# Forgetting scores in pairs of neighbouring PSUM banks: one maximum, one exponential and one sum for a query tile

## The chip, the cores and the metric

The kernel runs on one core of a Trainium2 chip. The time is device microseconds (us) of one execution, and the kernel before takes 1519.09 us, the median of three runs (1518.0 to 1522.42). TensorE (PE) multiplies matrices and writes its products to PSUM, which has eight banks of 128 partitions by 512 float32 numbers. VectorE (DVE) and ScalarE (ACT) read PSUM, GpSimd (POOL) works on SBUF alone, and SyncE (SP) issues the DMAs, in the order of one queue. Each of these engines works through its own instructions in order and waits for others through semaphores.

## The reference

One decoder layer for 1024 tokens of width 1024, all in float32: an mLSTM with 4 heads and forgetting attention with 8 heads of width 64 run side by side on the same normalised input; their outputs are projected, then come cross-attention into 256 memory tokens, a squared-ReLU MLP of width 4096, and a final norm. What the change touches is this:

```python
def forgetting_attention(q, k, v, lf):
    cT = jnp.cumsum(lf, axis=1).transpose(0, 2, 1)
    ...
        s = jnp.einsum('bqhd,bkhd->bhqk', qi, k, preferred_element_type=jnp.float32) * scale
        s = s + (ci[..., :, None] - cT[..., None, :])
        s = jnp.where(qpos[:, None] >= kpos[None, :], s, -jnp.inf)
        p = jax.nn.softmax(s, axis=-1)
        return jnp.einsum('bhqk,bkhd->bqhd', p.astype(v.dtype), v)
```

Queries are taken in tiles of 128. Tile i of a head sees (i + 1) * 128 keys, so the eight tiles of a head are 128, 256, ... 1024 wide.

## The kernel before

A float32 product is made of up to three products of rounded parts: `split` (L135) makes a high part on ACT (L138) and the rest on DVE (L139), and `mm3` (L190) issues the three matmuls (L192, L193, L194). Most of TensorE's time goes to these.

The stages in order: norm and projections; mLSTM heads 0 to 3 (`ml_project`, `ml_head`); the value projection of the forgetting heads (`token_major` with `fv_sink`, L1062); the forgetting heads; the rest of the output projection (`out_rest`); cross-attention; the MLP.

The forgetting heads are written out slot by slot. `slot` (L993) holds, in this order, the work of one step of several pipelines, and `in_order` (L148) ties each compute engine to that order. DMAs and everything outside the slots are placed by the scheduler that builds the program, by its own estimates. A slot has:

- on PE the transposes (`Values.turn`, L793) of up to four 128x128 blocks of probabilities into a `tp` bank (two such banks), with the causal mask (`mask`, L734) added to a score that is waiting for it; then the value products of the step two slots earlier (`Values.add`, L813) into the bank `ov`; then the scores of one part of one query tile (`Tile.score`, L754 and L755) into a bank `sc`; then filling products, below.
- on DVE the negated row maximum (`Tile.top`, L761) of the part scored one slot earlier; the rest of the cut of the transposed block (`Values.cut`, L139); reciprocals of the sums (L775); the sinks of filling products; half of the cuts of weights for these (`cut_half`, L967).
- on ACT the high part of `Values.cut` (L138), then the exponential of the part scored two slots earlier (`Tile.exp`, L767, which also sums), then the high part of a weight cut (L966).
- on POOL the division by the sum (`Tile.scale`, L778) and the other half of the weight cuts (L967).

A tile of up to 512 keys is one part and one `sc` bank; a wider one is two parts (640 keys: 384 and 256; otherwise 512 and the rest), scored in two slots. Each part has its exponential under a maximum of its own: L764 takes the smaller of the two negated maxima for the second part, L769 the factor between the two, L774 joins the sums, and L778 scales both parts. A head has 12 parts, so 12 slots; it has 12 steps of values, too. 13 slots with scores alone go ahead (`LEAD_`), and the values follow from then on, one step a slot.

The filling products (`filler`, L980) are 8 key units, 4 value units (two results each) and 16 units of the output projection, with the cost of a step written as 1.5 or 3.0 (12, 24 and 15 a unit). From the fourth slot with values on, a slot may take steps until the sum of costs reaches 3.6 a slot (L1041), and it stops where a result is complete (L1046 to L1048); the sink of that result runs in the next slot, behind the scores (L1036). Results go in turn to the banks `mm` and `m2`. What is left after the slots runs on its own (L1077).

The eight banks are `sc` x3, `mm`, `m2`, `tp` x2 and `ov`, from the start of the program to its end. The last mLSTM head takes `sc` for its column sums (L615) and for turning its factors into a row (`to_row`, L635); that row goes to DRAM and is read back by L261 and L637. Maxima and sums of a query tile lie in columns with three buffers (`col`, L82).

Of the kernel before, what the change touches and what calls it, by code (L numbers as in the profile page):

```python
# [44 lines left out]
def hybrid_layer(ctx: ExitStack, tc: tile.TileContext, a: dict, out: bass.AP):  # L45
    nc = tc.nc
    v, s, g = nc.vector, nc.scalar, nc.gpsimd

    pool = ctx.enter_context(tc.tile_pool(name="sb", bufs=1))
    psum = ctx.enter_context(tc.tile_pool(name="ps", bufs=1, space=PSUM))  # L50
    dram = ctx.enter_context(tc.tile_pool(name="dr", bufs=1, space=DRAM))

    count = [0]

    def name(tag):
        count[0] += 1
        return f"{tag}_{count[0]}"

    def sb(tag, shape, bufs, dt=F32):
# [25 lines left out]
    PBUFS = dict(sc=3, mm=1, m2=1, tp=2, ov=1)  # L85

    def ps_tile(tag):
        return psum.tile([P, 512], F32, tag=tag, name=name(tag), bufs=PBUFS[tag])

# [485 lines left out]
    mix = dram.tile([2, 2, P, KT, TH], F32, name="mix")  # L575
    facd = dram.tile([MLH, T], F32, name="facd")

    def ml_head(hd, q, k, og, num1, den1):
        fac = col("fac", 8)
        nums = []  # L580
        dens = col("dens", 8)
        sqs = col("sqs", 8)
        for hf in range(2):
# [44 lines left out]
        yield  # L628
        end = hd == MLH - 1
        fbs = [w2("a"), w2("d")] if end else [None, None]  # L630
        at = facd[hd : hd + 1]
        for hf in range(2):
            fb = fbs[hf] or w2("a")
            if hf == 0:
                to_row(fb, fac, 8, at, sc)  # L635
            if hf != end:
                load(fbs[1] or fb, at[:, TH:].broadcast_to([P, TH]))  # L637
# [73 lines left out]

    coming = []

    def fx_load(hd):
# [10 lines left out]
    def fx_step():  # L725
        if coming:
            dst, src = coming.pop(0)
            load(dst.bitcast(F32), src)

    masks = []  # L730

    def mask():
        while masks:
            nc.tensor.matmul(masks.pop(0), identb, causal, start=False, stop=True)  # L734

    class Tile:


        def __init__(self, hd, i, pt):
            self.hd, self.i, self.pt = hd, i, pt  # L740
            self.wid = (i + 1) * P

            step = 384 if self.wid == 640 else TH
            self.parts = [(c0, min(c0 + step, self.wid)) for c0 in range(0, self.wid, step)]
            self.mxs, self.dens = col("mx", 2), col("den", 2)
            self.ps = []

        def score(self, e):
# [3 lines left out]
            c2 = max(c1, c0 + 256)  # L752
            sp = sc()
            nc.tensor.matmul(sp[:, : c2 - c0], qs2[:, it], kl[:, c0:c2], start=True, stop=False)  # L754
            nc.tensor.matmul(sp[:, : c2 - c0], qs[:, it], kh[:, c0:c2], start=False, stop=c1 < self.wid)  # L755
            if c1 == self.wid:
                masks.append(sp[:, c1 - c0 - P : c1 - c0])
            self.ps.append(sp[:, : c1 - c0])

        def top(self, e):  # L760
            v.tensor_reduce(out=self.mxs[:, e : e + 1], in_=self.ps[e], axis=mybir.AxisListType.X, op=ALU.max, negate=True)  # L761
            if e:

                v.tensor_scalar(out=self.mxs[:, 1:2], in0=self.mxs[:, 1:2], scalar1=self.mxs[:, 0:1], scalar2=None, op0=ALU.min)  # L764

        def exp(self, e):
            s.activation(self.pt[:, slice(*self.parts[e])], self.ps[e], AF.Exp, bias=self.mxs[:, e : e + 1], accum_out=self.dens[:, e : e + 1])  # L767
            if e:
                s.activation(self.mxs[:, 0:1], self.mxs[:, 0:1], AF.Exp, bias=self.mxs[:, 1:2], scale=-1.0)  # L769

        def scale(self):
            den = self.dens[:, 0:1]
            if len(self.parts) > 1:
                v.scalar_tensor_tensor(out=den, in0=den, scalar=self.mxs[:, 0:1], in1=self.dens[:, 1:2], op0=ALU.mult, op1=ALU.add)  # L774
            v.reciprocal(den, den)  # L775
            for e, c in enumerate(self.parts):
                x = self.pt[:, slice(*c)]
                g.tensor_scalar(out=x, in0=x, scalar1=den, scalar2=self.mxs[:, 0:1] if e + 1 < len(self.parts) else 1.0, op0=ALU.mult, op1=ALU.mult)  # L778

# [75 lines left out]
    def value_steps():  # L855
        fvs = {0: fv_load(0)}
        for hd in range(FXH):
# [23 lines left out]

    late = []

# [106 lines left out]

    stores, topped = [], []

    def slot(values, until):  # L993
        with in_order():
            todo_ = late[:]
            late.clear()
            closing = bool(ended)
            sums = []
# [10 lines left out]
            while adds and not closing and len(adds) >= (LAG if x else 1):  # L1009
                y = adds.pop(0)  # L1010
                y.add()
                if y.last:
                    ended.append((y.hd, y.hf, y.ov))
                    break
            tops = scored[:]
            scored.clear()
            for t, e in tops:
                t.top(e)
            if x:
                x.cut()  # L1020
                adds.append(x)
            for f in sums:
                f()
            exps = topped[:]
            topped[:] = tops
            for t, e in exps:
                t.exp(e)
            while exped:
                exped.pop(0).scale()
            exped.extend(t for t, e in exps if e == len(t.parts) - 1)  # L1030
# [52 lines left out]
    banks[:] = ["mm", "tp", "m2", "tp"]  # L1083
    mix_fx = [mix_load(MLH + KX, KT, hf) for hf in range(2)]
# [635 lines left out]
```

## Time and profile before

| | |
|---|---|
| median of the runs | 1519.09 us (1518.0 to 1522.42) |
| the profiled execution | 1522.48 us; its span from the first to the last instruction 1520.3 us |
| granted TensorE clock | 0.997 |
| busy, share of the span | PE 99%, its weight loads 83%, DVE 72%, ACT 47%, POOL 29% |
| forgetting heads with values | from 392.3 us to about 579 us of the span |

PE's row counts the matmuls, whose ends are modelled and overlap; a matmul of 512 columns is shown with 0.39 us though the next starts 0.23 us later. So a wait shows as idle time only by what exceeds the matmul's modelled end. A number in square brackets in the list of instructions in order of time is the idle time of that engine before the instruction, with what ended it.

### The profile page before, as it was taken

The numbers are of one execution on the slowest core, as the hardware profiler recorded it, in microseconds if no ns is written. First come the engines' busy times: TensorE is split into PE (matmuls) and PEld (weight loads), VectorE is DVE, ScalarE is ACT, GpSimd is POOL, SyncE is SP. The second block draws the span as 40 slices with busy tenths as digits, with TensorE's granted clock in tenths as the row PEclk, the third lists the DMA queues.
The fourth block names the chain that finished last, engine by engine and source line by source line (L and its number), as shares of the span: only waits on it lengthen the run. The fifth ranks groups of instructions, "written<-read, shape, count | busy, mean of one in ns | idle before, by whom it ended". The sixth has DMA issues, their size and how long they took to land.

```text
span 1520.3 us, 21907 instructions
## 1 busy us (share of the span) xinstructions
PE 1501.2 (99%) x7708; PEld 1259.3 (83%) x7708; DVE 1097.8 (72%) x1741; ACT 717.2 (47%) x1345; POOL 438.5 (29%) x497
## 2 busy tenths in 40 slices
PE   9999999999999999999999999999999999999997
PEld 8888888889898888788888888888888888888887
DVE  7676676665798875844457888788887788777765
ACT  7343343334678763644344456565566432222124
POOL 0003030413455441011110033343344544333312
PEclk9999999999999999999999999999999999999998
DMA  6332333436887968833444436876775975555623
GB/s 206 117 113 91 114 102 124 132 126 172 260 246 222 285 205 313 300 123 122 134 137 157 165 118 237 278 274 243 261 265 214 361 262 222 222 222 215 254 84 111
DMA packets 118097, 296.71 MB, mean 195 GB/s; under 512 B 13138, under 2 KB 27788, under 8 KB 111844
## 3 DMA queue, kind: packets, MB, share of 16 engines
q1 hardware_dynamic: 117700, 295.21, 57.1%
q8 instruction: 60, 0.98, 0.3%
q14 instruction: 49, 0.40, 0.1%
q10 hardware_dynamic: 288, 0.11, 0.0%
HBM read 198.55 MB, written 96.72 MB: 194 GB/s over the span
## 4 chain that ended last, share of the span: by engine, by line
PE 61%; DMA 3%; DVE 2%; issue 1%; ACT 1%; SPq 0%; POOL 0%; POOLq 0%; DVEq 0%; ACTq 0%
PE sc L193 6%; PE sc L192 6%; PE sc L194 6%; PE tp L194 5%; PE tp L192 5%; PE tp L193 5%; PE m L193 4%; PE m L192 4%; PE m L194 4%; PE mm L194 3%; PE mm L193 3%; PE mm L192 3%; PE ov L192 2%; PE ov L194 2%; PE ov L193 2%; PE ov L813 1%
## 5 line engine op out<-in xcount | busy, mean ns | idle before, releaser
L193 PE MATMUL tp<-act,wh 128*128 128x512 f32 (+1 forms) x456 | 178.7, 392 | 0.0
L192 PE MATMUL tp<-act,wl 128*128 128x512 f32 (+1 forms) x456 | 178.5, 392 | 0.0
L194 PE MATMUL tp<-act,wh 128*128 128x512 f32 (+1 forms) x456 | 178.4, 392 | 0.0
L138 ACT ACTIVATE wh<-wr 128x1024 fp32r<-128x1024 f32 (+3 forms) x96 | 92.7, 967 | 99.5 <-PE tp L194 34.1
L139 DVE TENSOR_TENSOR wl<-wr,wh 128x1024 fp32r<-128x1024 f32 (+3 forms) x96 | 112.4, 1172 | 18.7 <-ACT wh L138 18.5
L192 PE MATMUL mm<-act,wl 128*128 128x512 f32 (+1 forms) x320 | 122.8, 384 | 0.0
L193 PE MATMUL mm<-act,wh 128*128 128x512 f32 (+1 forms) x320 | 122.5, 383 | 0.0
L194 PE MATMUL mm<-act,wh 128*128 128x512 f32 (+1 forms) x320 | 122.3, 382 | 0.0
L192 PE MATMUL m<-act,wl 128*128 128x512 f32 (+1 forms) x312 | 119.5, 383 | 2.2 <-DVE r_p L1094 2.2
L193 PE MATMUL m<-act,wh 128*128 128x512 f32 (+1 forms) x312 | 119.0, 382 | 1.0 <-DMA act<-mix 1.0
L194 PE MATMUL m<-act,wh 128*128 128x512 f32 (+1 forms) x312 | 119.0, 381 | 0.0
L192 PE MATMUL sc<-act,wl 128*128 128x512 f32 (+1 forms) x268 | 103.8, 387 | 0.0
L193 PE MATMUL sc<-act,wh 128*128 128x512 f32 (+1 forms) x268 | 103.6, 387 | 0.0
L194 PE MATMUL sc<-act,wh 128*128 128x512 f32 (+1 forms) x268 | 103.6, 387 | 0.0
L194 PEld LDWEIGHTS tp<-act,wh 128*128 128x128 f32 x456 | 85.7, 188 | 19.5
L192 PEld LDWEIGHTS tp<-act,wl 128*128 128x128 f32 x456 | 85.7, 188 | 18.9
L193 PEld LDWEIGHTS tp<-act,wh 128*128 128x128 f32 x456 | 85.8, 188 | 18.8
L1454 POOL TENSOR_TENSOR z<-wr 128x256 f32<-128x256 f32 x56 | 51.7, 944 | 149.3 <-DMA wr<-w_ff2q 107.6
L138 ACT ACTIVATE w<-wr 128x768 fp32r<-128x768 f32 (+2 forms) x31 | 25.5, 825 | 132.1 <-PE tp L194 68.1
L138 ACT ACTIVATE wh<-z 128x1024 fp32r<-128x1024 f32 (+2 forms) x55 | 52.5, 956 | 64.8 <-POOL z L1454 29.3
L139 DVE TENSOR_TENSOR wl<-z,wh 128x1024 fp32r<-128x1024 f32 (+2 forms) x55 | 64.6, 1174 | 11.7 <-ACT wh L138 11.5
L194 PEld LDWEIGHTS mm<-act,wh 128*128 128x128 f32 x320 | 60.1, 188 | 12.5
(679 smaller groups left out, 4199.4 us busy)
## 6 DMA issues: line engine op xcount, KB each, us to landing
act<-right SPq DMA_DIRECT2D x35, 1024.0 KB
right<-r_d SPq DMA_DIRECT2D x70, 256.0 KB
right<-w SPq DMA_DIRECT2D x56, 256.0 KB
wr<-w_ff2q SPq DMA_DIRECT2D x28, 512.0 KB
act<-fqk SPq DMA_DIRECT2D x48, 256.0 KB
wr<-w_in SPq DMA_DIRECT2D x20, 512.0 KB
wr<-w_ff SPq DMA_DIRECT2D x20, 512.0 KB
fqk<-r_p SPq DMA_DIRECT2D x32, 256.0 KB
```

Of the source, the lines that this page charges most:

```text
L138: s.activation(hi, src, AF.Copy)
L139: return v.tensor_tensor(out=lo, in0=src, in1=hi.bitcast(F32), op=ALU.subtract)
L192: nc.tensor.matmul(ps, w[1], x[0], start=first, stop=False, skip_group_check=more)
L193: nc.tensor.matmul(ps, w[0], x[1], start=False, stop=False, skip_group_check=more)
L194: nc.tensor.matmul(ps, w[0], x[0], start=False, stop=last, skip_group_check=more)
L813: nc.tensor.matmul(self.ov[:, c0:], self.fv[:, self.j], t[:, c0:], start=self.j == 0 and t is self.p[1], stop=self.last and t is self.p[0])
L1454: g.tensor_tensor(out=o, in0=x, in1=y, op=op)
```

## The change

While the forgetting heads run, the banks are laid out anew: `sc` x3 and `m2` give way to two pairs of neighbouring banks (`two_banks`), and both return when the slots are over. A query tile lies in one pair, so that one `top`, one `exp` and one `scale` take the whole of it, with one sum; L764, L769 and L774 go. Tiles 0 and 1 of a head share a pair, one bank each, and so do tiles 2 and 3. The 640-wide tile begins 128 columns into its pair, so that its parts are 384 and 256 as before; the matmuls of the scores are the same in number and width. A tile is passed on to `top` when its pair is complete, and its `exp` moves in the slot from behind the cut to ahead of the maxima.

Filling products have the bank `mm` alone. The sinks move from behind the scores to the head of the slot, and a slot in which such a sink runs takes no filling steps (`todo_`); the sum of costs is made up for later. The projection of the values of the forgetting heads has `mm`, `tp` and `tp`, and the last mLSTM head takes `ov` in place of `sc`. Some loads (later query and key rows, the first values, the memory tokens and the first two weights) are to be issued behind the read of the last mLSTM head's row.

```diff
+    four = [four_banks()]
...
     def ps_tile(tag):
-        return psum.tile([P, 512], F32, tag=tag, name=name(tag), bufs=PBUFS[tag])
+        from_ = four[0] if tag in ("sc", "m2") else psum
+        return from_.tile([P, 512], F32, tag=tag, name=name(tag), bufs=PBUFS[tag])
+
+    def two_banks():
+        return four[0].tile([P, 1024], F32, tag="pr", name=name("pr"), bufs=2)
...
-            ps = sc()
+            ps = (ov_ if end and hf else sc)()
...
-                to_row(fb, fac, 8, at, sc)
+                to_row(fb, fac, 8, at, ov_ if end else sc)
             if hf != end:
-                load(fbs[1] or fb, at[:, TH:].broadcast_to([P, TH]))
+                row_read[:] = [load(fbs[1] or fb, at[:, TH:].broadcast_to([P, TH]))]
...
+    four[0] = four_banks()
+    banks[:] = ["mm", "tp", "tp"]
...
             dst, src = coming.pop(0)
-            load(dst.bitcast(F32), src)
+            if fetched[0] > 16:
+                with tc.issue_after(row_read[0].ins):
+                    load(dst.bitcast(F32), src)
+            else:
+                load(dst.bitcast(F32), src)
+            fetched[0] += 1
...
-            step = 384 if self.wid == 640 else TH
-            self.parts = [(c0, min(c0 + step, self.wid)) for c0 in range(0, self.wid, step)]
-            self.mxs, self.dens = col("mx", 2), col("den", 2)
+            at = i % 2 * TH if i < 4 else P if self.wid == 640 else 0
+            cuts = [0, min(self.wid, TH - at % TH)] + [self.wid] * (self.wid > TH - at % TH)
+            self.parts = list(zip(cuts, cuts[1:]))
+            self.at = at
+            self.den = col("den")
+            self.top_ = col("mx")
...
+            if e == 0:
+                if self.i > 3 or self.i % 2 == 0:
+                    pair[:] = [two_banks()]
+                self.ps = pair[0][:, self.at : self.at + self.wid]
+                self.bank = pair[0]
+            sp = self.bank[:, self.at + c0 : self.at + c2]
...
+        def top(self):
+            v.tensor_reduce(out=self.top_, in_=self.ps, axis=mybir.AxisListType.X, op=ALU.max, negate=True)
+
+        def exp(self):
+            s.activation(self.pt, self.ps, AF.Exp, bias=self.top_, accum_out=self.den)
 
         def scale(self):
...
+            v.reciprocal(self.den, self.den)
+            g.tensor_scalar(out=self.pt, in0=self.pt, scalar1=self.den, scalar2=1.0, op0=ALU.mult, op1=ALU.mult)
...
-            todo_ = late[:]
+            todo_ = [f for f in late if f in sunk]
+            tails = [f() for f in late]
             late.clear()
+            sunk.clear()
...
+            exps = topped[:]
+            for t in exps:
+                t.exp()
             tops = scored[:]
             scored.clear()
-            for t, e in tops:
-                t.top(e)
+            for t in tops:
+                t.top()
...
                 part[0].score(part[1])
-                scored.append(part)
-            late.extend(filter(None, [f() for f in todo_]))
+                pending.append(part[0])
+                if part[1] or part[0].i in (1, 3):
+                    scored.extend(dict.fromkeys(pending))
+                    pending.clear()
+            late.extend(filter(None, tails))
...
-            while spent[0] < until:
+            while spent[0] < until and not todo_:
...
                     late.append(step[2])
+                    sunk.append(step[2])
                     break
...
-    load(hm.bitcast(F32), hmd)
-    banks[:] = ["mm", "m2"]
-    raw_load()
-    raw_load()
+    with tc.issue_after(row_read[0].ins):
+        load(hm.bitcast(F32), hmd)
+        raw_load()
+        raw_load()
+    banks[:] = ["mm"]
...
         slot(False, (n - DELAY) * RATE)
+    four[0] = four_banks()
+    banks[:] = ["mm", "tp", "m2", "tp"]
     for step in fill:
```

More of the change, by code (lines that the diff above doesn't have):

```diff
@@ L57, in name, with four_banks @@
         return f"{tag}_{count[0]}"
+    pool = ctx.enter_context(tc.tile_pool(name="sb", bufs=1))
+    psum = ctx.enter_context(tc.tile_pool(name="ps", bufs=1, space=PSUM))
+    scope = []
+    def four_banks():
+        if scope:
+            scope.pop().__exit__(None, None, None)
+        scope.append(tc.tile_pool(name=name("four"), bufs=1, space=PSUM))
+        return scope[0].__enter__()
+    dram = ctx.enter_context(tc.tile_pool(name="dr", bufs=1, space=DRAM))
     def sb(tag, shape, bufs, dt=F32):
@@ L712, in hybrid_layer @@
     coming = []
+    fetched = [0]
     def fx_load(hd):
@@ L734, in mask @@
             nc.tensor.matmul(masks.pop(0), identb, causal, start=False, stop=True)
+    pair = []
     class Tile:
@@ L766, in exp @@
[L766 to L769, printed above, removed]
-        def scale(self):
[L772 to L778, printed above, removed]
+            if e == 0:
[3 more added lines that the diff above has]
+                self.bank = pair[0]
@@ new lines, in score @@
+            sp = self.bank[:, self.at + c0 : self.at + c2]
+            nc.tensor.matmul(sp, qs2[:, it], kl[:, c0:c2], start=True, stop=False)
+            nc.tensor.matmul(sp, qs[:, it], kh[:, c0:c2], start=False, stop=c1 < self.wid)
+            if c1 == self.wid:
+                masks.append(self.ps[:, c1 - P :])
+        def top(self):
+            v.tensor_reduce(out=self.top_, in_=self.ps, axis=mybir.AxisListType.X, op=ALU.max, negate=True)
+        def exp(self):
+            s.activation(self.pt, self.ps, AF.Exp, bias=self.top_, accum_out=self.den)
@@ L880, in mix_tile @@
         return t[:, 0], t[:, 1]
-    late = []
+    late, sunk = [], []
     def key_unit(n):
@@ L1023, in slot @@
                 f()
-            exps = topped[:]
             topped[:] = tops
-            for t, e in exps:
-                t.exp(e)
             while exped:
                 exped.pop(0).scale()
-            exped.extend(t for t, e in exps if e == len(t.parts) - 1)
+            exped.extend(exps)
             fx_step()
```

23 lines of the change are left out of this document (6 added, 17 removed).

## The prediction

> **What bounds the kernel now.** I read the page's first part, the busy times by stage, PE's waits in this stage, and then the instructions in order of time. The page gives the whole:
>
> ```profile
> span 1520.3 us, 21907 instructions
> PE 1501.2 (99%) x7708; PEld 1259.3 (83%) x7708; DVE 1097.8 (72%) x1741; ACT 717.2 (47%) x1345; POOL 438.5 (29%) x497
> ```
>
> TensorE is the bound nearly everywhere. The change leaves every matmul of the scores as it was, so it can win only where PE waits, and lose only by new waits. The stage with values, in the view of busy time by stretch, and PE's waits in it:
>
> ```profile
> core 0: us, PE busy (x) PEld busy (x) DVE busy (x) ACT busy (x) POOL busy (x), PEclk, DMA share, GB/s
> 391.00:580.00 189.00, 184.38 (x1243) 164.83 (x1242) 159.86 (x377) 140.26 (x389) 93.46 (x145) 1.00 0.78 236
> ```
>
> ```profile
> PE sc L754 <- ACT act L767: 2.0, 3, 1.1
> PE m L193 <- DMA act<-mix: 1.0, 1, 1.0
> PE tp L793 <- DVE r_e L139: 0.8, 2, 0.4
> PE sc L754 <- ACT w L767: 0.4, 1, 0.4
> PE tp L793 <- DVE w L139: 0.3, 1, 0.3
> ```
>
> PE is idle for 189.00 - 184.38 = 4.6 us, at full clock. Of that, 2.4 us are scores that wait until an exponential gives up a bank, 1.1 us transposes that wait for a cut, and 1.0 us one wait for a load. DVE is at 85% and ACT at 74%: near PE, not past it. PE's instructions in order of time show how much of a wait the idle column leaves out:
>
> ```profile
> 393.17 0.39 PE L793 MATMUL tp<-ident,w 128*128 128x128 f32 x2
> 394.28 0.45 PE L754 MATMUL sc<-act 128*128 128x384 f32 x1 [0.73 <-ACT act L767]
> ...
> 394.74 0.27 PE L793 MATMUL tp<-ident,w 128*128 128x128 f32 x1
> ...
> 395.95 0.27 PE L793 MATMUL tp<-ident,w 128*128 128x128 f32 x1
> ...
> 396.87 0.60 PE L793 MATMUL tp<-ident,act 128*128 128x128 f32 x4
> 397.22 0.48 PE L813 MATMUL ov<-w,w 128*128 128x256 f32 x2
> 398.08 0.39 PE L754 MATMUL sc<-act 128*128 128x256 f32 x1 [0.38 <-ACT w L767]
> ...
> 398.43 0.28 PE L192 MATMUL m<-act,wl 128*128 128x256 f32 x1
> ...
> 458.88 0.50 PE L754 MATMUL sc<-act 128*128 128x512 f32 x1 [1.06 <-ACT act L767]
> ...
> 493.52 0.33 PE L793 MATMUL tp<-ident,w 128*128 128x128 f32 x1 [0.39 <-DVE r_e L139]
> ...
> 509.28 0.50 PE L193 MATMUL m<-act,wh 128*128 128x512 f32 x1 [0.98 <-DMA act<-mix]
> ```
>
> Four transposes at 396.87 let the next matmul start 0.35 us later, so the two at 393.17 should have let it start after about 0.18; it came after 1.11. The true wait is 0.93, shown as 0.73: about 0.2 more for each of the eight waits. All waits of the stage are then worth 4.6 + 8 x 0.2 = 6.2 us, 0.4% of the span. That is nearly all this change can win.
>
> **The change part by part.** *One operation for two, DVE.* The groups by form give
>
> ```profile
> L761 DVE TENSOR_REDUCE c_mx<-sc 128x1 f32<-128x512 f32 x34 | 23.2, 681 | 1.4 <-PE sc L734 1.4
> L764 DVE TENSOR_SCALAR c_mx<-c_mx 128x1 f32<-128x1 f32 x28 | 6.0, 214 | 1.0
> L774 DVE SCALAR_TENSOR_TENSOR c_den<-c_den,c_mx 128x1 f32<-128x1 f32 x26 | 5.7, 218 | 0.0
> L761 DVE TENSOR_REDUCE c_mx<-sc 128x1 f32<-128x128 f32 x6 | 1.7, 285 | 0.4 <-PE sc L734 0.4
> L936 DVE TENSOR_TENSOR r_p<-mm,r_p 128x512 f32<-128x512 f32 x2 | 1.4, 678 | 0.0
> ```
>
> A maximum costs (681 - 285) / 384 = 1.03 ns a column and 153 ns besides. The 32 wide tiles (4 a head, 8 heads) each save 153 + 214 + 218 = 585 ns: 18.7 us of DVE. An estimate for 1024 columns is 153 + 1056 = 1.21 us. *ACT:*
>
> ```profile
> L767 ACT ACTIVATE act<-sc,c_mx 128x512 f32<-128x512 f32 x29 | 19.9, 688 | 2.3 <-DVE c_mx L761 1.3 <-DVE c_mx L764 0.9
> L767 ACT ACTIVATION_READ_ACCUMULATOR act<-sc,c_mx 128x1 f32 x57 | 11.7, 206 | 0.0
> L769 ACT ACTIVATE c_mx<-c_mx 128x1 f32<-128x1 f32 x29 | 8.6, 295 | 0.0
> L767 ACT ACTIVATE act<-sc,c_mx 128x384 f32<-128x384 f32 x14 | 8.1, 581 | 1.1 <-DVE c_mx L764 0.9
> ```
>
> Here a column costs (688 - 581) / 128 = 0.84 ns and an instruction 260 ns, so a wide tile saves 260 + 206 + 295 = 761 ns, 24.4 us in all; an exponential of 1024 columns should take 1.12 + 0.21 us. POOL saves 32 instructions. None of this lies on PE's path itself: it is worth time only through the waits above.
>
> *The banks of the scores.* The slots are counted by the steps with values, 96 of them in the two groups of transposes:
>
> ```profile
> L793 PE MATMUL tp<-ident,act x208: 270/272/330, 396.9 to 577.0; 128*128 128x128 f32 x104
> L793 PE MATMUL tp<-ident,w x80: 270/273/328, 392.3 to 564.1; 128*128 128x128 f32 x80
> ```
>
> (288 transposes are 36 a head, for 12 steps.) So a slot is (578 - 392) / 96 = 1.94 us. Before, a part scored in slot n is reduced in n+1, has its exponential in n+2 behind the cut, and slot n+3 scores into its bank. From the start of n+2 that is transposes 0.4, cut 0.6, exponential 0.9, against 1.94 + 0.9 (transposes and value products ahead of the score): 0.9 us to spare. After, a pair is filled in slots n and n+1, reduced in n+2, its exponential stands first in n+3, and n+4 needs it: 0.4 + 1.21 + 1.33 and some 0.3 for hand-overs make 3.2 us, against 2 x 1.94 + 0.9 = 4.8. So 1.6 us to spare, with less work on both engines. I let these waits go, except the one at 458.88, which has another cause:
>
> ```profile
> 407.26 0.63 ACT L966 ACTIVATE wh<-wr 128x512 fp32r<-128x512 f32 x1 [1.21 <-DMA wr<-w_xk]
> 457.25 0.63 ACT L966 ACTIVATE wh<-wr 128x512 fp32r<-128x512 f32 x1 [3.04 <-DMA wr<-w_xv]
> 495.91 0.58 ACT L767 ACTIVATE w<-sc,c_mx 128x384 f32<-128x384 f32 x1 [1.12 <-POOL act L778]
> ```
>
> At 457.25 ACT has waited 3.04 us for a late weight, and everything behind that cut was late. The wider reserve takes about half of it. So: 394.28 and 398.08, 0.73 + 0.38 + 2 x 0.2 = -1.5; the other bank and transpose waits, 3.5 - 1.11 - 1.06 + 4 x 0.2 = -2.1; 458.88, half of 1.26, -0.6.
>
> [...]
>
> *Filling products on one bank.* A slot with a sink takes no filling. A sink is 0.41 to 0.7 us of DVE (L936 above), or one step on ACT and one on DVE, and it now stands first; the next filling comes one slot and a score later, over 2 us. So the single bank itself costs nothing while slots are full. In the last slots, without scores or values, nothing lies between a sink and the next product: 0.68 + 0.2 us, once, or nothing if the last cuts cover it. I take +0.5. The skipped step also gives the load before 509.28 one more slot to land: -1.2 at most, I take -1.0. What is not filled in the slots is done after them, at PE's own rate.
>
> *The queue of SP.* The first two weights and the later rows move behind the read of the last mLSTM head's row:
>
> ```profile
> 335.68 0.33 SPq L954 DMA_DIRECT2D wr<-w_xk  x1
> ...
> 373.36 0.43 SPq L637 DMA_DIRECT2D r_d<-facd  x1
> ...
> 403.37 5.44 SPq L954 DMA_DIRECT2D wr<-w_xk  x2
> ```
>
> A weight issued at 403.37 ended ACT's wait at 407.26, so it takes up to 3.9 us; issued behind 373.36, even after the memory tokens, it is there well before the first filling at 398.43. Zero. The three banks of the value projection, and `ov` in place of `sc`, cost zero too: PE has that projection's matmuls to go on with, and the scores no longer wait for the banks that the mLSTM head's last sums held.
>
> **Sum.** -1.5 - 2.1 - 0.6 - 1.0 + 0.5 = -4.7 us. The profiled execution took 1522.5 us, 3.4 above the median of the runs; it would be 1517.8, and against the median 1519.1 - 4.7 = 1514.4 us.
>
> **Rivals.** *Starved skips (slower).* In a slot without filling PE has little: 394.74 to 395.95 and 395.95 to 396.87, that is 1.21 and 0.92 us. DVE has 159.86 / 96 = 1.67 us a slot, after the change 1.67 - 0.19 = 1.47. If PE then waits each time for the cut, a skipped slot costs 0.26 to 0.55 us. There are 8 + 8 sinks of keys and values and, with 3.6 a slot over 93 slots, (335 - 192) / 15, some 10 of the output projection: 26 skips, 7 to 14 us. With half of the gains left, the time is 1524 to 1531, centre 1528. It decides as soon as DVE runs more than about half a slot behind PE; against it speaks that a cut has two slots until its product, and that the skipped steps come back in the next slots, where DVE catches up.
> [...]
>
> *Three columns for the sums (slower).* Tile 3 uses tile 0's column. Before, their exponential and division lay two slots apart, and even there an exponential waited 1.12 us for POOL (495.91, a neighbouring pair). Now tile 0 is divided in slot 4 and tile 3's exponential comes in slot 5, and it holds the cut behind it. At worst 8 heads x 1.3 = 10.6 us, so 1514.4 + 10.6 = 1525. It decides where the chain transposes 0.4, two maxima 1.23, cut 0.3, reciprocal, POOL 0.5, exponential 0.9 (3.5 us) passes two slots and 0.7; mean slots leave 1 us.
>
> *The waits only move (no change).* Late loads (457.25) and ACT's order make new waits as long as the old: 1519.
>
> **How the numbers follow.** The forecast's own range is the terms at their ends: from all 6.2 gone, and the one at the start of the next stage too,
>
> ```profile
> 643.34 0.50 PE L192 MATMUL m<-act,wl 128*128 128x512 f32 x1 [2.21 <-DVE r_p L1094]
> ```
>
> to a third of them: 1510.7 to 1517. I give it 0.62; it straddles 0.3% (4.6 us, about what a measurement of this kernel can tell from no change), 0.38 beyond and 0.24 within. Waits that move have 0.04, starved skips 0.20, the columns 0.09, and a load that is late after all 0.05. So faster 0.38, same 0.28, slower 0.34, and the range runs from 1510 to 1529.
>
> **What would show it.** Right: PE's idle time between 391 and 580 falls from 4.6 to about 1.5 us, with DVE's busy time down by some 19 us and ACT's by 24; the groups of L761 and L767 have 64 members with forms up to 1024; no wait at 394 or 509. Starved skips would show as many waits of transposes or value products for a cut, a few tenths each, behind every sink; the columns as exponentials that wait for POOL once a head. The prediction is wrong if PE's idle time there grows, or if a wait for a load appears at the first filling.

## The result and the profile after

The kernel after takes 1527.05 us, the median of nine runs (1523.36 to 1529.71), beside 1520.78 us for the kernel before on the same chip (nine runs, 1518.0 to 1524.69). The ratio is 1.0035, 95% interval 1.0021 to 1.0049: about 5.3 us slower, where 4.7 us faster was forecast. (Here and below the ratio comes from all runs and need not be that of the two medians.) The forecast's own 1510.7 to 1517 did not hold the time; the range of 1510 to 1529, which takes in the rivals, did. The profiled execution took 1527.77 us, 5.3 more than that of before. Its page begins

```profile
span 1526.0 us, 21717 instructions
PE 1506.3 (99%) x7708; PEld 1259.2 (83%) x7708; DVE 1080.8 (71%) x1645; ACT 703.7 (46%) x1249; POOL 429.4 (28%) x465
```

VectorE's 1097.8 us became 1080.8, ScalarE's 717.2 became 703.7, and the span grew by 5.7 us. The view of busy time by stretch, with the columns that the prediction shows:

```profile
391.00:580.00 189.00, 183.92 (x1230) 161.46 (x1229) 141.35 (x291) 127.54 (x300) 84.07 (x115) 1.00 0.79 242
```

In the stage with values VectorE's busy time fell by 159.86 - 141.35 = 18.5 us, as forecast. PE's idle time did not fall from 4.6 to 1.5 us: it is 189.00 - 183.92 = 5.1. PE's waits in this stage, by line and what was waited for (total us, times, longest us):

```profile
PE tp L813 <- DVE r_e L153: 2.5, 7, 0.7
PE mm L206 <- DVE r_a L915: 0.7, 1, 0.7
PE tp L813 <- DVE w L153: 0.6, 2, 0.4
PE mm L206 <- DVE r_p L915: 0.4, 1, 0.4
```

The scores that waited for an exponential (2.4 us) are gone, and so is the wait for the mix load (1.0 us). In their place stand nine waits of transposes for the cut and two of filling products for the sink of their one bank. Two of the nine in order of time, the first in a slot ahead of the filling (which begins with the fourth), the second in a skipped slot:

```profile
392.99 0.42 PE L785 MATMUL pr<-act 128*128 128x384 f32 x1
393.25 0.34 PE L786 MATMUL pr<-act 128*128 128x384 f32 x1
394.02 0.33 PE L813 MATMUL tp<-ident,w 128*128 128x128 f32 x1 [0.44 <-DVE r_e L153]
...
476.03 0.40 PE L786 MATMUL pr<-act 128*128 128x512 f32 x1
476.75 0.66 PE L813 MATMUL tp<-ident,act 128*128 128x128 f32 x4 [0.32 <-DVE r_e L153]
```

The score at 392.99 waits for nothing (its like at 394.28 waited 0.73 before), but the transposes right behind it do. Six of the nine waits stand like the one at 476.75, in a slot without filling that comes after the filling has begun (412.78, 434.64, 462.80, 476.75, 503.29, 526.23): 0.2 to 0.4 us each, 1.9 us together. So waits of starved slots show in six of the 26 skipped slots that the prediction counts, not behind every sink. What the wide instructions cost is in the groups by line (shortest, median and longest ns, first and last start):

```profile
L791 DVE TENSOR_REDUCE c_mx<-pr x64: 273/748/1225, 356.5 to 560.3; 128x1 f32<-128x128 f32 x8, 128x1 f32<-128x256 f32 x8, 128x1 f32<-128x384 f32 x8, 128x1 f32<-128x512 f32 x8
...
L794 ACT ACTIVATE act<-pr,c_mx x32: 792/954/1119, 363.7 to 561.6; 128x640 f32<-128x640 f32 x8, 128x768 f32<-128x768 f32 x8, 128x896 f32<-128x896 f32 x8, 128x1024 f32<-128x1024 f32 x8
```

The widest maximum takes 1.23 us and the widest exponential 1.12, where 1.21 and 1.12 were worked out. The length of the stage is read from the group of its transposes, here of after (before: 392.3 to 577.0, as the prediction shows):

```profile
L813 PE MATMUL tp<-ident,act x208: 270/272/331, 396.4 to 579.2; 128*128 128x128 f32 x104
L813 PE MATMUL tp<-ident,w x80: 270/272/332, 391.9 to 565.7; 128*128 128x128 f32 x80
```

From the first to the last that is 187.3 us, against 184.7. So 2.6 us of the loss lie in the stage. The rest lies behind it. There the same two views show a wait of 1.0 us that before does not have, one of 2.5 us near the place where before waits 2.2 (643.34 in the prediction), and, in one stretch, a lower granted clock (the third number from the end, 0.91; before 1.00):

```profile
PE sc L207 <- DVE act L156: 2.5, 1, 2.5
PE tp L206 <- DVE wl L153: 1.0, 1, 1.0
```

```profile
640.00:660.00 20.00, 17.29 (x72) 13.42 (x71) 13.13 (x22) 8.29 (x12) 1.02 (x1) 0.91 0.80 291
```

The wait of 1.0 us begins in the last slots. PE's instructions in order of time:

```profile
579.73 0.28 PE L833 MATMUL ov<-r_d,w 128*128 128x256 f32 x1
579.85 0.39 PE L206 MATMUL tp<-act,wl 128*128 128x512 f32 x1
...
583.11 0.39 PE L208 MATMUL tp<-z,wh 128*128 128x512 f32 x1
583.33 0.40 PE L833 MATMUL ov<-w,w 128*128 128x256 f32 x2
```

Fifteen matmuls of left-over filling products went into a free bank of the transposes ahead of the last value product. The sums of the last head close later for it (ScalarE copies them at 585.20 us, before at 579.57), and SyncE's queue, which issues in order, is late with all that follows (issues in order of time; before, the last mix load went out at 586.00 and the weight at 590.64):

```profile
589.22 0.43 SPq L849 DMA_DIRECT2D mix<-r_f  x1
...
593.40 1.55 SPq L894 DMA_DIRECT2D act<-mix  x2
...
596.88 0.59 SPq L194 DMA_DIRECT2D wr<-w_out_b  x1
```

That weight is the one PE waits for near 605.

### The profile page after: what moved, and what is told of

The parts are those of the page before. It is cut to its first block, busy times and chain, and to the rows that moved or that the text cites. A ratio compares the mean times of both kernels' runs of the same rounds, so it can differ in the third digit from the quotient of the medians.

```text
span 1526.0 us, 21717 instructions
## 1 busy us (share of the span) xinstructions
PE 1506.3 (99%) x7708; PEld 1259.2 (83%) x7708; DVE 1080.8 (71%) x1645; ACT 703.7 (46%) x1249; POOL 429.4 (28%) x465
## 4 chain that ended last, share of the span: by engine, by line
PE 62%; DMA 3%; DVE 2%; issue 1%; ACT 0%; SPq 0%; POOL 0%; POOLq 0%; DVEq 0%; ACTq 0%
PE sc L207 6%; PE sc L208 6%; PE sc L206 6%; PE tp L206 5%; PE tp L208 5%; PE tp L207 5%; PE mm L208 4%; PE mm L206 4%; PE mm L207 4%; PE m L206 3%; PE m L207 3%; PE m L208 3%; PE ov L206 2%; PE ov L208 2%; PE ov L207 2%; PE ov L833 1%
## 5 line engine op out<-in xcount | busy, mean ns | idle before, releaser
L206 PE MATMUL tp<-act,wl 128*128 128x512 f32 (+1 forms) x468 | 183.4, 393 | 1.0 <-DVE wl L153 1.0
L207 PE MATMUL tp<-act,wh 128*128 128x512 f32 (+1 forms) x468 | 183.5, 392 | 0.0
L208 PE MATMUL tp<-act,wh 128*128 128x512 f32 (+1 forms) x468 | 183.2, 392 | 0.0
L206 PE MATMUL mm<-act,wl 128*128 128x512 f32 (+1 forms) x364 | 136.5, 375 | 0.9 <-DVE r_a L915 0.7
L207 PE MATMUL mm<-act,wh 128*128 128x512 f32 (+1 forms) x364 | 136.1, 374 | 0.0
L208 PE MATMUL mm<-act,wh 128*128 128x512 f32 (+1 forms) x364 | 136.1, 374 | 0.0
L208 PEld LDWEIGHTS tp<-act,wh 128*128 128x128 f32 x468 | 88.0, 188 | 20.0
L207 PEld LDWEIGHTS tp<-act,wh 128*128 128x128 f32 x468 | 88.0, 188 | 19.2
L206 PE MATMUL m<-act,wl 128*128 128x512 f32 (+1 forms) x256 | 101.8, 398 | 0.2 <-DVE r_p L1123 0.2
L208 PE MATMUL m<-act,wh 128*128 128x512 f32 (+1 forms) x256 | 101.1, 395 | 0.0
L207 PE MATMUL m<-act,wh 128*128 128x512 f32 (+1 forms) x256 | 101.0, 395 | 0.0
L206 PEld LDWEIGHTS mm<-act,wl 128*128 128x128 f32 x364 | 68.4, 188 | 13.8 <-POOL wl L988 1.0
L208 PEld LDWEIGHTS mm<-act,wh 128*128 128x128 f32 x364 | 68.4, 188 | 12.9
```

The source lines that it names most:

```text
L206: nc.tensor.matmul(ps, w[1], x[0], start=first, stop=False, skip_group_check=more)
L207: nc.tensor.matmul(ps, w[0], x[1], start=False, stop=False, skip_group_check=more)
L208: nc.tensor.matmul(ps, w[0], x[0], start=False, stop=last, skip_group_check=more)
```

## The experiments

Each ratio is to the kernel before on the same chip; its median is 1520.78 to 1523.21 us on the chips used, so ratios are compared and not medians. "Stage" is the start of the last transpose less that of the first, in one profiled execution each. In every kernel of the table 1215 to 1218 matmuls lie between them, so a longer stage holds longer waits and no more work.

| kernel | median us | ratio, 95% interval | stage us |
|---|---|---|---|
| before | 1520.78 | 1 | 184.7 |
| after | 1527.05 | 1.0035 (1.0021 to 1.0049) | 187.3 |
| fill_alone: before, with all of the filling part | 1529.68 | 1.0064 (1.0046 to 1.0083) | 191.8 |
| skip_alone: before, with the skipped step | 1528.25 | 1.0038 (1.0024 to 1.0052) | 191.6 |
| sinks_first: before, with the sinks first | 1523.18 | 1.0011 (1.0000 to 1.0023) | 187.0 |
| no_skip: after, without the skipped step | 1541.44 | 1.0132 (1.0118 to 1.0146) | 200.0 |
| no_order: after, without the new order of SyncE's queue | 1530.06 | 1.0061 (1.0045 to 1.0078) | 189.8 |
| order_before: before, with that order | 1522.84 | 0.9999 (0.9988 to 1.0011) | 185.7 |
| cols: after, with more columns | 1526.00 | 1.0035 (1.0022 to 1.0048) | 189.2 |
| mended: after, with the end mended | 1523.29 | 1.0017 (1.0003 to 1.0030) | 187.6 |
| mended_before: before, with the later release and an edit meant to load the weight earlier | 1518.51 | 0.9972 (0.9961 to 0.9984) | 184.0 |

**The filling part, taken apart.** fill_alone puts into the kernel before the single bank, the sinks at the head of the slot, the skipped step and, as in after, the transposes' banks for the filling left over behind the slots; the scores stay narrow.

```diff
-            todo_ = late[:]
+            todo_ = [f for f in late if f in sunk]
+            tails = [f() for f in late]
             late.clear()
+            sunk.clear()
-            while spent[0] < until:
+            while spent[0] < until and not todo_:
-    banks[:] = ["mm", "m2"]
+    banks[:] = ["mm"]
```

> The kernel before with the filling part of the change alone: the bank mm for all filling products in the slots, the sinks at the head of the slot, and the slot of a sink without filling steps; scores, parts, banks sc and loads are as before (m2 stands unused there). If the loss lies in this part (skipped slots in which PE waits for a cut, and fillings that wait for their one bank), it is slower than the kernel before by 3 to 8 us, with PE waits for cuts directly behind scores. If the loss lies in the pairs or in what follows the slots, it is within 2 us of the kernel before.

1.0064, about 9.7 us: this part by itself loses more than the whole change, so the rest of the change gains 0.29% (1.0064 to 1.0035; the intervals of the two leave about 0.23% either way). The stage is 7.1 us longer than before. PE's largest waits in it:

```profile
PE sc L754 <- ACT act L767: 4.5, 6, 3.0
PE sc L754 <- ACT w L767: 3.6, 6, 2.1
```

These are 8.1 us of scores that wait for an exponential, where before has 2.4 and after none; waits for cuts, which the expectation named, are 0.4 us. Is it the bank or the skip? no_skip takes the skip out of after:

```diff
-            while spent[0] < until and not todo_:
+            while spent[0] < until:
```

> The changed kernel, in which a slot with a sink may take filling steps again; the bank is still mm alone and the sink still at the head. If the skipped slot starves PE, the waits for a cut directly behind a score (some 2.8 us in seven places of the changed kernel) go, and the time falls by 1 to 3 us; if the skip is what keeps the single bank from stopping PE, waits of the filling products for a sink (2.0 us in four places) grow to 26 x 0.5 = 13 us and the time rises by 5 us or more.

1.0132. With one bank and no skip, PE waits for the sinks; its largest waits in the stage:

```profile
PE mm L206 <- DVE r_a L915: 3.8, 3, 2.4
PE mm L206 <- DVE r_p L915: 3.3, 3, 1.4
...
PE mm L206 <- DVE r_a L156: 2.4, 3, 1.0
PE mm L206 <- DVE r_b L957: 2.4, 3, 0.9
```

So one bank needs the skip. What the skip costs where it isn't needed, with two banks and late sinks:

```diff
-            while spent[0] < until:
+            while spent[0] < until and not skip_:
```

(`skip_` holds the sinks of groups finished in the slot before.)

> The kernel before with the skipped step alone: a slot in which the sink of a finished filling group is emptied takes no filling; the two filling banks, the late sinks and the narrow scores stay. Theory 'the skipped steps starve TensorE': this alone gives most of the 0.64% of the filling part, the ratio is 1.004 to 1.007, and PE's waits in the stage grow by 5 us or more with transposes or scores behind the skipped slots. Theory 'the single bank is what costs, the skip only moves filling to behind the slots': the ratio stays within 0.15% of 1.

1.0038, just below the 1.004 to 1.007 expected, and a stage of 191.6 us, 6.9 more than before and as long as fill_alone's. PE's idle time that shows in it grows from 4.6 to 8.7 us, by 4.1 and not by 5. Where PE waits:

```profile
PE sc L754 <- ACT act L767: 5.1, 5, 3.5
PE sc L754 <- ACT w L767: 2.2, 4, 1.3
PE tp L793 <- DVE r_e L139: 1.1, 2, 0.8
```

So the price of the skip is shown, and how it comes about only in part. With narrow scores PE waits at the next score, whose bank an exponential still holds, and seldom at the transposes. Two of these waits, 3.48 us at 463.62 and 1.34 at 498.92, stand behind late weights (w_xv and w_xk) for which ScalarE waited 5.28 and 2.07 us; before has 1.06 at the first (458.88) and nothing at the second. That is 3.8 of the 6.9 us in this execution; the rest lies in shorter waits. fill_alone has the same two places, with 2.97 and 2.06 us. No run shows whether the skip makes the weights late: sinks_first, below, skips nothing, and in its profile ScalarE waited 5.09 us for w_xv and PE 3.3 with it. The sinks' place alone:

```diff
-            todo_ = late[:]
+            tails = [f() for f in late]
             late.clear()
...
-            late.extend(filter(None, [f() for f in todo_]))
+            late.extend(filter(None, tails))
```

> The kernel before with the sinks moved to the head of the slot alone (two banks, no skipped step). Theory 'the sink ahead of the cut holds the cut up': the transposes wait 0.3 to 0.7 us longer in the 26 slots with a sink where VectorE is late; the ratio is 1.001 to 1.004. Theory 'the order of the sinks is free while two banks are there': the ratio stays within 0.1% of 1.

1.0011, hardly told from 1. If the parts add, 0.38 + 0.11 leave some 0.15% of fill_alone's 0.64 for the single bank and the end of the slots, which these intervals do not resolve.

**The slots without filling.** Both kernels with the filling held back in the slots (`slot(True, 0)` and `slot(False, 0)`); all of it is still done.

> The kernel before with no filling products in the slots: they all run behind the slots. This shows the pipeline of scores and values by itself, where PE is not the bound, as the base of the next run. The stage from the first transpose to the last value product, 187 us before, should shrink to some 140 to 165 us, held by DVE (160 us busy with the filling's sinks and weight cuts, of which some 30 us leave the stage). The whole should be slower than the kernel before by 5 to 30 us, by what PE now waits there.

> The changed kernel with no filling products in the slots, against the run before this one: the pairs of banks and the single maximum, exponential and sum by themselves. If the wide operations are the gain that the prediction reckoned (18.7 us less of DVE, 24.4 us less of ACT), the stage is shorter than without the change by 5 to 19 us. If the pairs themselves are the loss (two banks held for longer than three single ones), the stage is as long as without the change or longer, and PE waits at the scores.

Before: 1537.67 us, 1.0110 (1.0094 to 1.0126). After: 1589.19 us, 1.0442 (1.0422 to 1.0462). The pair is no clean comparison: before, the second filling bank is free and left-over products are put between the slots all the same (1150 matmuls from 391 to 580 us, beside 1243 with filling); after, with one bank, fewer are (920, beside 1230), and the rest are done behind the slots. But the second one shows what slots without filling cost, in PE's waits of the stage:

```profile
PE tp L813 <- DVE r_e L153: 17.7, 31, 1.5
PE tp L813 <- DVE w L153: 4.8, 14, 0.7
```

22.5 us in 45 waits for the cut: 0.5 us where PE waits, but it does not wait in every slot. From the first transpose to the last (392.1 to 550.2) PE is idle for 158.1 - 127.3 = 30.8 us, 0.32 us for each of the 96 slots, near the low end of the 0.26 to 0.55 of the starved skips.

**The wide scores.** More columns, the cut ahead of the exponential, and the banks dealt out otherwise (two for filling, one for the transposes, and late sinks without a skip):

```diff
-            self.den = col("den")
-            self.top_ = col("mx")
+            both_ = col(("mx", "den")[i % 2], 2)
+            self.den, self.top_ = both_[:, 0:1], both_[:, 1:2]
```

> The kernel after, with twice as many columns for the maxima and sums of the rows (they alternate between two names of three buffers, so a column is free again six tiles later and not three). Rival 'three columns for the sums': the exponentials' waits for GpSimd, 1.9 us in four waits in the profile after, go, and the ratio falls from 1.0035 towards 1.000 or below. If the columns do not matter, those waits go or stay without any effect on TensorE, and the ratio stays within 0.1% of 1.0035.

1.0035, as after: the exponentials' four waits for GpSimd (1.9 us in after) are gone, and nothing is gained. Its profile had a wait of 3.5 us for the cut at 464.3, behind the same late weight, for which ScalarE waited 5.17 us there and 1.88 in after.

> The changed kernel with the cut of the transposed block ahead of exponential and maximum in each slot (before, the cut stood ahead of the exponential and behind the maximum). PE's waits in the stage are now waits of transposes for a cut (some 3 us shown, 5 us with what the modelled ends hide). If a wide operation ahead of the cut is what makes the cut late, these waits go and the time falls by 2 to 5 us, unless the scores then wait for their pairs. If the skipped slots alone make them, they stay.

1532.32 us, 1.0075 (1.0063 to 1.0088): the scores wait for their pairs again, 5.8 us. So exponential first, as after has it, is better by 0.4%.

> The kernel after, with its eight banks dealt out otherwise: one bank for the transposes and two for the filling products in the stage with values, and with the sinks and the filling as they were before (sinks late in the slot, no skipped step). The wide scores stay. Theory 'the single filling bank with its skipped slots costs the 0.6%, and the wide scores by themselves win about 0.3%': if one bank for the transposes is enough, no transposes wait behind skipped slots and the ratio falls below 1, to about 0.997. Theory 'the bank was free, something in the wide scores costs': the ratio stays at 1.0035. If the one bank of the transposes is itself short, transposes wait for the cut of the slot before, in nearly all of 96 slots, and with 0.1 to 0.3 us each the ratio rises to 1.01 or more; then this run shows only that the eight banks cannot be dealt out better.

1560.64 us, 1.0258 (1.0245 to 1.0271). One bank is too few for the transposes: they wait 21.5 us up to 580 us, nearly all of it for a cut. This is the third case of its expectation, so it says only that the eight banks cannot be dealt out like this.

**SyncE's queue.** The three `issue_after` blocks taken out of after, and put into before:

```diff
-        with tc.issue_after(row_read[0].ins):
-            fvs = {0: fv_load(0)}
+        fvs = {0: fv_load(0)}
```

> The kernel after without the three places that put loads behind the read of the last mLSTM head's row in the queue of SyncE (the first weights and the memory tokens, the first values, the later rows of queries and keys). The forecast costed them at nothing. If so, the ratio stays within 0.1% of 1.0035 and the profile shows no new wait before 420 us. If the new order helped, waits for loads or for the row of the last head appear between 355 and 400 us and the ratio rises above 1.005; if it hurt, the ratio falls below 1.002.

1.0061. The first value slots of no_order, in order of time:

```profile
392.60 0.28 PE L782 MATMUL pr<-act 128*128 128x256 f32 x1
393.94 0.33 PE L809 MATMUL tp<-ident,w 128*128 128x128 f32 x1 [1.06 <-DVE r_c L156]
...
397.40 0.48 PE L809 MATMUL tp<-ident,w 128*128 128x128 f32 x1 [2.50 <-DVE r_e L153]
```

and what VectorE waited for just ahead of them:

```profile
392.74 0.75 DVE L655 SCALAR_TENSOR_TENSOR r_f<-r_f,vec,r_a 128x512 f32<-128x512 f32 x1 [5.17 <-DMA r_a<-facd]
```

The last mLSTM head's row is read at 385.9 instead of 376.7, its products fall into the first value slots, and the cuts stand behind them. In fill_alone and skip_alone, which have the old banks, it is read at 372.3 and 372.9, so the delay comes with the new banks; no run separates the pairs, the three banks of the value projection and `ov`. (after and no_order differ by 0.26%, and their intervals leave some 0.22% either way.)

> The kernel before with the new order of SyncE's queue alone (first weights, memory tokens, first values and later rows behind the read of the last mLSTM head's row). Theory 'the order only repays what the pairs cost the last head': in the kernel before the row is read at 373.36 already, so the ratio stays within 0.1% of 1. Theory 'the order is a gain of its own': the ratio is 0.997 to 0.998, and half or more of what the change lost could have been had without it.

0.9999: in the kernel before the order brings nothing, as its row is read at 373 anyway. It repairs a delay of the change itself. Without it the wide scores gain nothing that can be measured (fill_alone 1.0064, no_order 1.0061).

**Behind the slots.** Four edits of after: no filling in the last slots (bare_tail); the left-over filling ordered behind the last value product (end_first); the next stage's load released by the last tile written and not the last but two (late_kx_after); and the last two together (mended, in which a weight was to go ahead of the mix load, too). Each profile shows one execution; those of end_first (1520.42 us) and mended (1521.96) are among the fastest of twelve.

```diff
-    for step in fill:
+    with tc.issue_after(added[0].ins):
+        for step in fill:
...
-        if hf == 1 and n == KT - 3:
+        if hf == 1 and n == KT - 1:
```

> The changed kernel with no filling steps in the slots behind the last values, so that the last value products, the closing copy and the last stores of mixed heads are not held up by filling. In the changed kernel the last value product starts 4.2 us later than before, the load of the mixed heads for the rest of the output projection is issued some 7 us later, and PE waits 1.0 us for that projection's first weight. If the late end of the slots is what loses time afterwards, the waits near 605 and 646 us shrink and the time falls by 1 to 5 us. If what follows the slots loses time for another reason, it stays within 1 us of the changed kernel.

1524.14 us, 1.0027 (1.0016 to 1.0039); the left-over filling still goes ahead of the last value product, and the wait near 605 stays (1.0 us); the one near 646 is gone in its profile (19.85 of the 20 us from 640 to 660 busy, clock 1.00).

> The kernel after, with every matmul of the filling that is left over behind the slots ordered behind the last value product; nothing else is changed. In the profile after, 15 of those filling matmuls stood between the last value products (579.85 to 583.33), the copy of the last sums came at 585.20 (before: 579.57), the load of the last mix tiles at 593.40 (before: 586.00), and TensorE waited 1.0 us near 605 for the weights behind that load. Theory 'the end of the stage is part of the loss': the last value product comes 1.5 to 2.5 us earlier, the load of the mix near 591, the wait near 605 shrinks below 0.3 us; TensorE pays up to 1 us for the last cut, so the ratio falls from 1.0035 to about 1.003. Theory 'the loss lies in the slots alone': the wait near 605 stays or moves, and the ratio stays at 1.0035 or grows by the wait for the cut.

1525.62 us, 1.0031 (1.0017 to 1.0044). In its profile the waits near 605 and 646 and the lower clock are gone (PE busy for all of 580 to 700, clock 1.00), but the ratio gains nothing that can be told.

> The changed kernel with the loads of keys and values of the memory tokens held back until the last tile of the rest of the output projection is stored (the last but two before). Those loads share the DMA queues with the loads that the last sums wait for. If they make the wait of 2.47 us near 646 us and this wait is what lowers TensorE's clock behind it (matmuls of 512 columns then start 0.43 us apart, not 0.23, for some 3.5 us), both go together and the time falls by 3 to 5 us. If the clock falls for another reason, the slow matmuls stay.

1527.11 us, 1.0050 (1.0037 to 1.0064): the wait at 646 shrinks to 1.5 us, but the one near 605 is 1.9 and has a lower clock behind it (0.91 from 600 to 620 us).

> The kernel after with three edits behind the slots: the left-over filling ordered behind the last value product, the first weight of the second part of the output projection loaded ahead of the last mix tiles in the queue of SyncE, and the load for the next stage released by the last tile written instead of the last but two. Theory 'about 3 of the 5.3 us lie behind the slots (a wait of 1.0 us near 605, and 2.5 us of lower clock behind a wait of 2.5 us at 646), 2 in them': both waits fall below 1 us, the clock stays at 1.00 from 580 to 700, and the ratio falls to 1.0010 to 1.0015. Theory 'the end is only a symptom': the waits move on and the ratio stays above 1.003.

1.0017. Both waits and the lower clock are gone (one wait of 0.4 us, for a cut, is left from 580 to 700; clock 1.00). (The weight did not go ahead of the mix load: it was issued at 594.53, the load at 588.08.) The same cure for the kernel before, first by the release alone, then with the weight too:

> The same hold in the kernel before, which shows a wait of 2.21 us at that place and no slow matmuls. If the clock depends on the wait, only that wait goes: the time falls by 1 to 2.5 us. If the loads do not make the wait, nothing changes.

1519.27 us, 0.9983 (0.9974 to 0.9993); the wait of 2.21 us is gone (PE busy for all of 580 to 700).

> The kernel before with two edits behind the slots: the first weight of the second part of the output projection is loaded ahead of the last mix tiles, and the load for the next stage is released by the last tile written. The second alone gave 0.9983. The kernel before has no wait near 605, so the first should add nothing: 0.998 to 0.9985, and the kernel after, mended likewise, stays 0.3% above it. If it comes out above 0.999, the earlier weight holds back something else.

0.9972, the lowest of all, though the weight did not go ahead here either (issued at 589.67, the mix loads at 585.51 and 586.41; before 590.64). Mended much alike (the left-over filling is ordered in mended alone), after stands 0.45% above before (1.0017 to 0.9972). So the end of the stage is a place where the profiled execution lost time, but not what makes the change slower: the kernel before had as much to gain there.

## Why the prediction was wrong

- *The banks of the scores* were right in mechanism: the scores' waits at 394 and 398 are gone, and the wide instructions last as worked out. Wide scores with the queue's order gain 0.29%, 4.4 us, against 1.5 + 2.1 + 0.6 = 4.2 forecast; the interval spans 1 to 8 us, so that the two agree is partly luck. (The 1.0 us of the load at 509.28 belongs to the next step: that wait is gone in fill_alone, too.)
- *Filling products on one bank* is the step that failed: "So the single bank itself costs nothing while slots are full", with +0.5 us for the last slots and -1.0 for the load. The part costs 0.64%, 9.7 us (fill_alone), and the skipped step alone 0.38%, 5.8 us. The sentence looked at the filling product, which comes two microseconds after its sink, and not at PE in the slot in which nothing is filled. In the profiled execution of skip_alone the loss in the stage lies partly in short waits and partly (3.8 of 6.9 us) in waits behind late weights; whether the skip makes the weights late stays open.
- *Starved skips*, held at 0.20, is the rival that came nearest: 7 to 14 us were worked out for 26 skips, 9.7 measured for the part, and its time of 1524 to 1531 holds 1527. That the price fits is partly luck: its sign, a wait for a cut behind every sink, shows in six places of after, and in fill_alone the waits stand at the scores, two of the largest behind late weights. What spoke against it, that skipped steps come back in later slots, is no help: PE was the bound (busy for 99% of the span), and the time it idles in one slot does not return (the stage of skip_alone is 6.9 us longer). With one bank and no skip (no_skip) PE waits for the sinks, 11.9 us in the twelve waits listed above, and the ratio is 1.0132.
- *The queue of SP*, "Zero", was right for the sum only because the order repays 0.26% (1.0061 to 1.0035) that the new banks ahead of the slots would have cost, the three banks and `ov`, also "zero", among them. The trace of before could not show it: there the row was read in time.
- *Three columns* fell by cols. *Waits only move* is what PE's idle time in the stage looks like (4.6 and 5.1 us), but gain and loss come from different parts, and the loss of the filling part (0.64%) is larger than their difference.
- Not foreseen at all: the left-over filling that overtook the last value product, "done after them, at PE's own rate".
- VectorE's saving was as forecast; ScalarE's busy time fell by 140.26 - 127.54 = 12.7 us, not 24. The instructions went (389 to 300), and the sum of their durations fell by 24.4 us in the same window (174.6 to 150.2), as forecast. But neighbouring durations overlap: in before an exponential of 0.70 us at 497.84 is followed by the read of its sum at 498.41, after 0.57 us. Busy time counts such an overlap once, and the forecast counted it twice.
- Open: how the loss divides. In three executions with the stage of before (before, late_kx_before, mended_before) the stage takes 183.5 to 184.7 us, in four with that of after (after, late_kx_after, end_first, mended) 186.5 to 187.6, 2.9 us more on the mean; where the rest of the 5.3 us lies is not settled. One weight load may have part in it. ScalarE's wait for w_xv near 461 is 1.3 to 5.2 us in eight kernels with wide scores and the whole filling part, with up to 3.5 us of PE's; 2.1 to 3.5 in four with the filling of before; 4.8 to 6.1 in fill_alone, skip_alone, sinks_first and no_skip. No experiment removed that wait.

## What to carry to other kernels

Where TensorE is the bound, filler work is not free to move: a slot that was told to skip its filling let TensorE run into the next dependency (skip_alone, 1.0038), so price the empty slot by the shortest chain that it must then wait for, times the number of skips, and see which loads come late with it. A buffer taken from one use must be priced in the use that loses it, and first by a kernel that makes only that loss (here fill_alone, 1.0064). A cure for one place should be tried on the old kernel too before it is counted for the new one (late_kx_before, 0.9983; order_before, 0.9999).

## What the runs showed of the hardware

In some of the profiled executions a single wait of TensorE was followed by a lower clock. In after, behind the wait of 2.47 us at 646, matmuls of 512 columns started 0.43 us apart, where they start 0.23 apart at a granted clock of 1.00:

```profile
646.46 0.50 PE L207 MATMUL sc<-act,wh 128*128 128x512 f32 x1 [2.47 <-DVE act L156]
...
648.25 0.63 PE L207 MATMUL m<-act,wh 128*128 128x512 f32 x1
648.68 0.63 PE L208 MATMUL m<-act,wh 128*128 128x512 f32 x1
...
650.81 0.50 PE L207 MATMUL m<-act,wh 128*128 128x512 f32 x1
```

The slow stretch lasted about 3 us (647.66 to 650.81), so it cost nearly half of that; the granted clock was 0.91 from 640 to 660 us. In no_order a wait of 1.76 us (648.09) had the same behind it (0.91 in the same stretch), in late_kx_after one of 1.87 (605.47) and in sinks_first one of 3.04 (604.06; 0.91 from 600 to 620 us in both). But 2.21 us in before (643.34), 1.97 in cols (647.69) and 2.5 in fill_alone had nothing: in all three the clock was 1.00 from 640 to 660 us. So the length of the wait alone does not decide: 1.76 us had the lower clock behind it, 2.5 us did not. What decides was not tested.
